# A gated delta rule woven by hand into the projections of one encoder layer

## The chip, the core and the metric

The kernel runs on one core of a Trainium2 chip. The metric is device time of one execution in microseconds (us). The kernel before takes 2366.16 us, the median of three runs (2364.62 to 2370.51).

## The reference, cut to what matters

The program is a two-layer encoder for two groups of rows, 256 and 512, that share all weights; side by side they make T = 768 columns of 1024 features. The first (even) layer normalises, projects, runs three branches (a Hyena long convolution, a gated DeltaNet in both directions with 8 heads of 128, an attention over a memory) and projects back; the second (odd) layer has attention branches and is not touched. What matters here is the DeltaNet and the input projections that feed it and the Hyena branch:

```python
qkv = silu(centred_depthwise_conv(z_qkv, gdn_conv_w))        # 5 taps
q = l2_normalize(q) * d ** -0.5;  k = l2_normalize(k)
# per head and direction, in chunks of 64 rows
a = where(strict, einsum('id,jd->ij', k * beta, k) * decay, 0)
t_inv = triangular_solve(a + eye, eye)                       # unit lower triangle
u, w = t_inv @ (v * beta), t_inv @ (k * beta * exp(g))
# scan over the chunks
v_new = u_i - w_i @ state
o_i = (q_i * exp(g)) @ state + qk_i @ v_new
state = state * exp(g_last) + k_decayed_i.T @ v_new
y_b = rms_norm(o_forward + o_backward, gdn_norm_g) * silu(g_gdn)
# Hyena's share of the projections: 3 taps, then gates
x0, x1, v_hy = split(centred_depthwise_conv(z_hy, hy_conv_w) + hy_conv_b)
y_a = x0 * long_conv(v_hy * x1) * silu(g_hy)
```

## The kernel before, in words

The even layer's middle part holds 64 projections: 32 for the DeltaNet (q, k, v and gate of 8 heads) and 32 for Hyena (x0, x1, v and gate of 8 column blocks). One projection gives 128 features by 768 columns. It runs 8 steps over the 1024 inputs; in each step three products (high x high, low x high, high x low: L256, L258, L260) go over 512 and then 256 columns, so it has 48 products. In this text an eighth is one such step of six products. A projection's output lies in a PSUM tile `pp` of two banks; there are two such tiles. All small products share four more banks, the tiles `pb`.

After its projection q, k and v go through five taps on VectorE (L455: eight instructions, two for each of four taps, after a first one on ScalarE at L448) and a silu; the gate and one Hyena projection of four have a silu alone (L328); the other Hyena projections have four tap instructions. The silu or the last tap frees the `pp` tile.

For each head there are four pieces of small work:

- front: 18 transposes (L332), norms, six products of 256 columns (L554) from which `P` and `A` are scaled (L558), and a gather of `A`'s diagonal blocks over DRAM into `B` and `W` (L572 to L575).
- inverse: 30 steps on VectorE, two instructions each (L589, L591), each dependent on the last; then a copy of `B` (L592) and a scatter over DRAM (`wd`) into `TTN` by 16 transfers (L596, L602).
- levels: the inverse is widened from 32 to 64 to 128 rows on TensorE with evacuations between (L618, L620, L625, L627, L629, L636, L638, L642).
- scan and output: four steps for four chains (two directions, two row groups); in each `v` (L667, L670), `wv` and `w2` (L678, L680, L684), the output and the state (L686 to L693), then six transposes.

The string `ORDER` fixes in which order the pieces are written: F is the projections of a head, its front and its inverse; B is levels and scan; X and U are two Hyena projections each. The order on each engine is not this one: a list scheduler places every instruction by priority and an own estimate of when its inputs are ready, and so mixes small products between the projection's products, at the grain of a single product. At run time every engine takes its instructions strictly in the order so fixed and waits where an input is late.

Of the kernel before, what the change touches and what calls it, by code (L numbers as in the profile page):

```python
# [18 lines left out]
T = 768  # L19
# [204 lines left out]
ORDER = "F0 X0 F1 U0 B0 X1 F2 U1 B1 X2 F3 U2 B2 X3 F4 U3 B3 X4 F5 U4 B4 X5 F6 U5 B5 F7 X6 B6 U6 B7 X7 U7"  # L224


class K:
# [216 lines left out]
    def conv(self, out, ps, taps, tile_ix, width, bias=None):  # L444
# [13 lines left out]

# [25 lines left out]

    def gdn_proj(self, p, h, n0):
        we = self.a["we"]
        kq = p.tile([128, 2, T], F32, tag="kq", name="kq", bufs=2)
        for i, nm in enumerate(("q", "k", "v")):
            w = self.wload(we[n0 + i], self.wp, 128)
            ps = self.proj(w)  # L490
            acc = p.tile([128, T], F32, tag="cv", name="cv", bufs=2)
            self.conv(acc, ps, V_GCW, 8 * i + h, 5)
            if nm == "v":
                vT = p.tile([128, T], F32, tag="vt", name="vT")
                dst = vT
# [4 lines left out]
        ps = self.proj(w)  # L500
        sg = p.tile([128, T], F32, tag="sg", name="sg", bufs=2)
        self.silu2(p, sg, ps)
        return kq, vT, sg

    def gdn_front(self, p, h, E, kq, vT, sg):
# [8 lines left out]
        for which in range(2):  # L514
            sqs = p.tile([128, 128], F32, tag="vs", name="sqs")
            for t0, n in ((0, 4), (4, 2)):
# [6 lines left out]
                if which == 0:  # L523
                    nc.scalar.activation(out=kt[:, t0:t0 + n, :], in_=v3, func=AF.Copy)
        nc.vector.tensor_scalar_add(ss, ss, 4.0 * EPS)
# [14 lines left out]
        for t0, n in ((0, 4), (4, 2)):  # L540
            pt = self.bank()
            for t in range(n):
                self.transpose(pt[:, 128 * t:128 * t + 128], vT[:, 128 * (t0 + t):128 * (t0 + t) + 128])
            nc.vector.tensor_tensor(out=nv[:, t0:t0 + n, :], in0=pt[:, :128 * n].rearrange("p (t d) -> p t d", t=n),
                                    in1=nk[:, t0:t0 + n, None].to_broadcast([128, n, 128]), op=ALU.mult)

        self.mark("g.AP%d" % h)
        Pm = p.tile([128, 2, TT, 128], F32, tag="P", name="P", bufs=2)
        for t0 in range(0, TT, 2):
# [7 lines left out]
            for o, x, e in ((Pm[:, 0, t2], 1, E[0][:, t2]), (Pm[:, 1, t2], 1, E[1][:, t2]), (A[:, t2], 0, A[:, t2])):  # L557
                nc.vector.tensor_tensor(out=o, in0=v[:, :, x], in1=e, op=ALU.mult)  # L558

# [17 lines left out]
        return dict(kq=kq, sg=sg, kt=kt, nv=nv, rs=rs, ed=ed, A=A, Pm=Pm)  # L577

    def gdn_inv(self, p, h):
# [6 lines left out]
        for m in range(1, 31):  # L586
# [4 lines left out]
            nc.vector.tensor_tensor(out=W[:, :m, m + 1:], in0=W[:, :m, m + 1:], in1=tmp, op=ALU.add)  # L591
        nc.scalar.activation(out=B, in_=W.rearrange("p a b -> p b a"), func=AF.Copy)  # L592
# [11 lines left out]
    def gdn_back(self, p, h, kq, sg, kt, nv, rs, ed, A, Pm):  # L604
# [11 lines left out]
        for t in range(TT):  # L616
            for d, e, l in els:
                mm(ps[sl(l), 32 * t:32 * t + 32], A[sl(e), t, sl(l)], tn[d][sl(e), t, sl(e % 2)], tile_position=(32 * e, 32 * l))  # L618
        x = p.tile([128, TT, 64], F32, tag="x64", name="x32", bufs=1)
        nc.vector.tensor_scalar_mul(x[:, :, :32], tv(ps, 32), -1.0)  # L620
        pd = [self.bank() for _ in range(2)]
        for t in range(TT):
# [3 lines left out]
            for d, e, l in (els[0], els[3]):  # L626
                mm(pd[d][sl(l), c], tt[d][sl(l), t, sl(l)], x[sl(l), t, :32], tile_position=(32 * l, 32 * l))  # L627
        for d, e, l in (els[0], els[3]):
            nc.vector.tensor_copy(tn[d][sl(l), :, sl(e % 2)], tv(pd[d], 32)[sl(l)])  # L629
        for d, e, l in els:  # L630
            nc.scalar.activation(out=tt[d][sl(e), :, sl(l)], in_=tv(pd[d], 32)[sl(e)], func=AF.Copy)
        hf = [(0, slice(0, 64), slice(64, 128)), (1, slice(64, 128), slice(0, 64))]
        ps = self.bank()
        for t in range(TT):
            for d, eq, lq in hf:
                mm(ps[lq, 64 * t:64 * t + 64], A[eq, t, lq], tn[d][eq, t, :], tile_position=(eq.start, lq.start))  # L636
        x = p.tile([128, TT, 64], F32, tag="x64", name="x64", bufs=1)
        nc.vector.tensor_scalar_mul(x, tv(ps, 64), -1.0)  # L638
        ps = self.bank()
# [3 lines left out]
        for d, eq, lq in hf:  # L643
            nc.scalar.activation(out=tt[d][eq, :, lq], in_=tv(ps, 64)[eq], func=AF.Copy)
        yield
# [11 lines left out]
        for step in range(4):  # L657
            for si, (d, seq) in enumerate(seqs):
                if step >= len(seq):
                    continue  # L660
                t = seq[step]
                ts = slice(128 * t, 128 * t + 128)
                if step == 0:
                    v1 = nv[:, t, :]
                else:
                    ps = self.bank()
                    mm(ps[:, :128], kq[:, 0, ts], S[si])  # L667
                    mm(ps[:, 128:256], kq[:, 1, ts], S[si])
                    v1 = p.tile([128, 128], F32, tag="v1", name="v1", bufs=3)
                    nc.vector.scalar_tensor_tensor(out=v1, in0=ps[:, :128], scalar=self.gneg[:, d, t, h:h + 1], in1=nv[:, t, :], op0=ALU.mult, op1=ALU.add)  # L670
                    eg = self.gex[:, 3 * d, t, h:h + 1]
                    if t not in seen:
                        nc.scalar.activation(out=o[:, t, :], in_=ps[:, 128:256], func=AF.Copy, scale=eg)
                        seen.add(t)
                    else:
                        nc.vector.scalar_tensor_tensor(out=o[:, t, :], in0=ps[:, 128:256], scalar=eg, in1=o[:, t, :], op0=ALU.mult, op1=ALU.add)
                ps = self.bank()
                mm(ps[:, :128], TTN[:, d, t, 0:128], v1)  # L678
                w = p.tile([128, 128], F32, tag="wv", name="wv", bufs=2)
                nc.vector.tensor_copy(w, ps[:, :128])  # L680
                last = step == len(seq) - 1
                if not last:
                    w2 = p.tile([128, 128], F32, tag="w2", name="w2", bufs=2)
                    nc.scalar.activation(out=w2, in_=ps[:, :128], func=AF.Copy, scale=ed[:, d, t:t + 1])  # L684
                ps = self.bank()
                mm(ps[:, :128], Pm[:, d, t, :], w)  # L686
                if not last:
                    mm(ps[:, 128:256], kt[:, t, :], w2)
# [12 lines left out]
                yield  # L701

# [9 lines left out]
        y = sg  # L712
        for t0, n in ((0, 4), (4, 2)):
# [4 lines left out]
            nc.vector.scalar_tensor_tensor(out=y[:, cs], in0=pt[:, :128 * n], scalar=self.vec(V_GN), in1=sg[:, cs], op0=ALU.mult, op1=ALU.mult)  # L718
        nc.scalar.dma_start(out=self.y[8 + h], in_=y)


    def hy_proj(self, p, c, n0, halves=(0, 1)):
        nc = self.nc

        def part(i):
            w = self.wload(self.a["we"][n0 + i], self.wp, 128)
            ps = self.proj(w)
            t = p.tile([128, T], F32, tag="hy", name="hy", bufs=2)
            if i < 3:
                self.conv(t, ps, V_HCW, 8 * i + c, 3, bias=self.vec(V_HCB + 8 * i + c))  # L730
            else:
                self.silu2(p, t, ps)
            return t
        for i, j, dst in [((1, 2, self.ud[c]), (0, 3, self.xd[c]))[x] for x in halves]:
            t0, t1 = part(i), part(j)
            nc.gpsimd.tensor_tensor(out=t1, in0=t1, in1=t0, op=ALU.mult)
            nc.scalar.dma_start(out=dst, in_=t1)

# [611 lines left out]
def trunk(tc, a, outs, dbg=None):  # L1350
    nc = tc.nc
    dbg = dbg or {}
    with ExitStack() as ctx:
# [24 lines left out]
        with ExitStack() as gd:  # L1378
# [32 lines left out]
            def front(i):  # L1411
                if i > 0:
                    E = k.gdn_decay(p, i)
                k.mark("gproj")
                g = k.gdn_proj(p, i, 4 * i)
                if i == 0:
                    k.mark("gates")
                    k.gdn_gates(p)
                if i == 0:
                    E = k.gdn_decay(p, 0)  # L1420
                st[i] = k.gdn_front(p, i, E, *g)
                k.gdn_inv(p, i)

            def hy(c, halves=(0, 1)):
                k.mark("hproj")
                k.hy_proj(p, c, 32 + 4 * c, halves)
            def back(i):
                st["o", i] = k.gdn_back(p, i, **st.pop(i))
                for _ in range(13):
                    next(st["o", i])  # L1430

            def out(i):
                for _ in st["o", i]:
                    pass
            run = {"F": front, "B": back, "U": lambda c: hy(c, (0,)), "X": lambda c: hy(c, (1,))}
            for ch in ORDER.split():
                i = int(ch[1])
                run[ch[0]](i)
                if ch[0] == "B" and i < 7:
                    out(i)  # L1440
# [4 lines left out]
            def hyconv():  # L1445
# [4 lines left out]
                out(7)  # L1450
# [113 lines left out]
```

## Time and profile before

| what | value |
|---|---|
| median of three runs | 2366.16 us |
| profiled execution | 2362.44 us |
| its span | 2360.7 us (1.7 us lie around it) |
| TensorE busy | 2213.2 us, 94% |
| VectorE busy | 1414.8 us, 60% |
| ScalarE busy | 896.5 us, 38% |
| GpSimd busy | 433.9 us, 18% |

Shares are means over the whole span. The part that the change touches lies between about 273 and 1051 us of the span; the rows further down are from there. A busy TensorE may run at a granted clock of 0.50 instead of 1.00, so its waits and its clock have both to be read.

### The profile page before, as it was taken

The numbers are of one execution on the slowest core, as the hardware profiler recorded it, in microseconds if no ns is written. First come the engines' busy times: TensorE is split into PE (matmuls) and PEld (weight loads), VectorE is DVE, ScalarE is ACT, GpSimd is POOL, SyncE is SP. The second block draws the span as 40 slices with busy tenths as digits, with TensorE's granted clock in tenths as the row PEclk, the third lists the DMA queues.
The fourth block names the chain that finished last, engine by engine and source line by source line (L and its number), as shares of the span: only waits on it lengthen the run. The fifth ranks groups of instructions, "written<-read, shape, count | busy, mean of one in ns | idle before, by whom it ended". The sixth has DMA issues, their size and how long they took to land. (4 is left out here: it accounts for less than half of the span.)

```text
span 2360.7 us, 35185 instructions
## 1 busy us (share of the span) xinstructions
PE 2213.2 (94%) x13648; PEld 1855.1 (79%) x13648; DVE 1414.8 (60%) x3236; ACT 896.5 (38%) x1888; POOL 433.9 (18%) x303
## 2 busy tenths in 40 slices
PE   8999898889999998889999979999999999999897
PEld 6788776777878887777778858988888877778785
DVE  6775387785776867758651264236555577664414
ACT  6333544435345344322142352122222344443423
POOL 2344242223233231223300140000000000000002
PEclk9999999999999998999999989999999999999898
DMA  7442223222223222246362342111111211111613
GB/s 247 138 158 96 73 84 78 82 82 73 78 73 90 78 62 60 67 165 222 113 197 62 102 135 90 54 56 58 52 46 43 77 50 50 40 62 46 203 63 107
DMA packets 122705, 218.98 MB, mean 93 GB/s; under 512 B 49592, under 2 KB 62297, under 8 KB 122282
## 3 DMA queue, kind: packets, MB, share of 16 engines
q1 hardware_dynamic: 102746, 171.86, 23.9%
q10 hardware_dynamic: 19568, 44.04, 5.0%
q8 instruction: 107, 1.75, 0.3%
q0 software_dynamic: 224, 0.83, 0.1%
q14 instruction: 60, 0.49, 0.1%
HBM read 174.43 MB, written 42.25 MB: 92 GB/s over the span
## 5 line engine op out<-in xcount | busy, mean ns | idle before, releaser
L256 PE MATMUL pp<-hhi,w 128*128 128x512 f32 (+1 forms) x2032 | 558.5, 348 | 20.5 <-DVE cv L455 9.6
L258 PE MATMUL pp<-hlo,w 128*128 128x512 f32 (+1 forms) x2032 | 553.6, 347 | 0.0
L260 PE MATMUL pp<-hhi,w 128*128 128x512 f32 (+1 forms) x2032 | 545.9, 344 | 0.0
L256 PEld LDWEIGHTS pp<-hhi,w 128*128 128x128 f32 (+1 forms) x2032 | 321.2, 190 | 68.3 <-issue 17.2
L258 PEld LDWEIGHTS pp<-hlo,w 128*128 128x128 f32 (+1 forms) x2032 | 319.4, 190 | 47.9 <-issue 6.6
L260 PEld LDWEIGHTS pp<-hhi,w 128*128 128x128 f32 (+1 forms) x2032 | 318.0, 189 | 44.8 <-issue 2.7
L1013 PE MATMUL pp<-yh,wo 128*128 128x256 f32 (+1 forms) x1152 | 274.1, 348 | 17.3 <-DVE wo L241 9.0
L240 ACT ACTIVATE w<-wr 128x1024 fp32r<-128x1024 f32 x155 | 163.3, 1053 | 296.6 <-PE pp L260 247.3
L241 POOL TENSOR_TENSOR w<-wr,w 128x1024 fp32r<-128x1024 f32 (+1 forms) x65 | 155.3, 2389 | 462.5 <-ACT w L240 305.4
L1013 PEld LDWEIGHTS pp<-yh,wo 128*128 128x128 f32 x1152 | 191.5, 195 | 48.8 <-ACT yh L240 11.5
L241 DVE TENSOR_TENSOR w<-wr,w 128x1024 fp32r<-128x1024 f32 x90 | 113.6, 1263 | 140.3 <-ACT w L240 140.1
L241 DVE TENSOR_TENSOR wo<-wor,wo 128x640 fp32r<-128x640 f32 (+1 forms) x76 | 62.0, 817 | 191.5 <-ACT wo L240 191.4
L1013 PE MATMUL pp<-yl,wo 128*128 128x512 f32 (+1 forms) x576 | 170.2, 349 | 0.2
L241 POOL TENSOR_TENSOR xk<-raw,xk 128x512 fp32r<-128x512 f32 x8 | 10.8, 1356 | 751.7 <-ACT xk L240 751.7
L455 DVE SCALAR_TENSOR_TENSOR cv<-pp,vecs,cv 128x510 f32<-128x510 f32 (+1 forms) x192 | 107.4, 605 | 24.7 <-ACT cv L448 24.7
L1013 PEld LDWEIGHTS pp<-yl,wo 128*128 128x128 f32 x576 | 100.1, 194 | 17.3 <-DVE yl L241 1.9
L240 ACT ACTIVATE wo<-wor 128x640 fp32r<-128x640 f32 (+1 forms) x76 | 52.0, 686 | 159.1 <-PE pp L1013 146.4
L589 DVE TENSOR_TENSOR Bt<-W,B 48x30 f32<-48x30 f32 (+14 forms) x240 | 98.5, 410 | 4.2 <-DMA B<-bd 2.5
L591 DVE TENSOR_TENSOR W<-W,Bt 48x30 f32<-48x30 f32 (+14 forms) x240 | 97.9, 408 | 1.8
L1022 POOL TENSOR_TENSOR oacc<-oacc,osq 128x768 f32<-128x768 f32 (+2 forms) x15 | 24.0, 1601 | 279.6 <-ACT osq L1018 279.6
L455 DVE SCALAR_TENSOR_TENSOR hy<-pp,vecs,hy 128x511 f32<-128x511 f32 x96 | 55.6, 606 | 30.6 <-ACT hy L448 30.2
L686 PE MATMUL pb<-wv,P 128*128 128x128 f32 x192 | 42.4, 303 | 20.9 <-DVE wv L680 20.9
(322 smaller groups left out, 3736.4 us busy)
## 6 DMA issues: line engine op xcount, KB each, us to landing
wr<-we SPq DMA_DIRECT2D x72, 512.0 KB, 3.5
wr<-wog SPq DMA_DIRECT2D x30, 512.0 KB, 3.6
wor<-weo SPq DMA_DIRECT2D x40, 320.0 KB, 3.2
wr<-wqk SPq DMA_DIRECT2D x24, 512.0 KB, 3.3
wor<-woo SPq DMA_DIRECT2D x36, 256.0 KB, 3.0
yr<-ye SPq DMA_DIRECT2D x20, 384.0 KB, 3.9
dec<-dec ACTq DMA_DIRECT2D x8, 768.0 KB, 4.3
fd<-F ACTq DMA_DIRECT2D x8, 768.0 KB, 3.5
```

Source lines behind the costliest of these rows:

```text
L240: nc.scalar.activation(out=hi, in_=src, func=AF.Copy)
L241: (lo_eng or self.lo_eng or nc.vector).tensor_tensor(out=lo, in0=src, in1=hi.bitcast(F32), op=ALU.subtract)
L256: mm(ps[:, s:e], wh, rhs_hi[:, s:e], start=first, stop=False)
L258: mm(ps[:, s:e], wh, rhs_lo[:, s:e], start=False, stop=False)
L260: mm(ps[:, s:e], wl, rhs_hi[:, s:e], start=False, stop=last)
L455: nc.vector.scalar_tensor_tensor(out=out[:, lo:hi], in0=ps[:, lo + s:hi + s], scalar=self.vec(taps + 24 * j + tile_ix), in1=out[:, lo:hi], ...
L589: nc.vector.tensor_tensor(out=tmp, in0=W[:, :m, m:m + 1].to_broadcast([48, m, n]), in1=B[:, m:m + 1, m + 1:].to_broadcast([48, m, n]), op= ...
L591: nc.vector.tensor_tensor(out=W[:, :m, m + 1:], in0=W[:, :m, m + 1:], in1=tmp, op=ALU.add)
L686: mm(ps[:, :128], Pm[:, d, t, :], w)
L1013: mm(ps[:, s:e], w[:, wi, j, :], y[order[i], g], start=i == 0 and x == 0, stop=i == nk - 1 and x == 2)
L1022: nc.gpsimd.tensor_tensor(out=acc[:, s:e], in0=acc[:, s:e], in1=sq[:, s:e], op=ALU.add)
```

## The change

`ORDER` goes. The projections become a generator (`big`) that stops after each eighth; the taps, the inverse and the small work become generators too. One loop runs `big`; after each eighth it deals out two instructions of taps or silu from a queue (`k.post`), one inverse step of each head whose inverse has begun, and small groups of products at a rate of six per five eighths. TensorE's order is then exactly the order in which the loop writes (`tc.manual_schedule`); the other engines stay with the scheduler. The levels and the scan of head i-1 follow directly on the front of head i. The scan is regrouped: in each step all chains' `v`, then all `wv`, then all outputs and states. Some buffers grow (`kq` 2 to 3, `v1` 3 to 4, `wv` and `w2` 2 to 4); `pp` and `pb` don't. Each engine has the same instructions as before; only their order differs.

```diff
-ORDER = "F0 X0 F1 U0 B0 X1 F2 U1 B1 X2 F3 U2 B2 X3 F4 U3 B3 X4 F5 U4 B4 X5 F6 U5 B5 F7 X6 B6 U6 B7 X7 U7"
+    def proj_g(self, whl):
+        ps = self.pp.tile([128, 1024], F32, tag="pp", name="pp")[:, :T]
+        for k in range(8):
+            self.mm3(ps, whl, 0, self.hhi[k], self.hlo[k], k, k == 0, k == 7, ((0, 512), (512, 768)))
+            yield
+        return ps
...
+        for i, nm in enumerate(("q", "k", "v")):
+            w = self.wload(we[n0 + i], self.wp, 128)
+            ps = yield from self.proj_g(w)
+            self.post.append(post(i, nm, ps))
...
+        for i, j, dst in ((0, 3, self.xd[c]), (1, 2, self.ud[c])):
+            ts = []
+            for x in (i, j):
+                ps = yield from self.proj_g(self.wload(self.a["we"][n0 + x], self.wp, 128))
+                ts.append(p.tile([128, T], F32, tag="hy", name="hy", bufs=2))
+                self.post.append(post(x, ps, ts[-1]))
+            self.post.append(gate(*ts, dst))
...
+            def small():
+                for i in range(8):
+                    while i not in fronts:
+                        yield
+                    E, q = fronts.pop(i)
+                    sg = q.pop("sg")
+                    st[i] = dict((yield from k.gdn_front(p, i, E, **q)), sg=sg)
+                    inv.append(k.gdn_inv(p, i))
+                    if i > 0:
+                        yield from k.gdn_back(p, i - 1, **st.pop(i - 1))
+                for _ in inv[7]:
+                    yield
+                yield from k.gdn_back(p, 7, **st.pop(7))
+
+            def big():
+                hys = chain(*(k.hy_proj(p, c, 32 + 4 * c) for c in range(8)))
+                for i in range(8):
...
+                    q = yield from k.gdn_proj(p, i, 4 * i)
...
+                    while "sg" not in q:
+                        run(k.post)
+                    fronts[i] = E, q
+                    if i > 0:
+                        for _ in range(24):
+                            next(hys)
+                            yield
+                yield from hys
...
+            with tc.manual_schedule(engines={mybir.EngineType.PE}):
+                for n, _ in enumerate(big()):
+                    if n % 8 == 7:
+                        while len(k.post) > 2:
+                            run(k.post)
+                    run(k.post)
+                    run(k.post)
+                    for g in inv:
+                        next(g, None)
+                    while done < n * 6 // 5:
+                        done += 1
+                        next(sm, None)
```

Lines shift with the new code: L455 becomes L462, L589 and L591 become L609 and L611, L618 becomes L639, L625 becomes L648, L636 becomes L662, L678 becomes L710, L686 becomes L726, L256 to L260 become L255 to L259, L328 becomes L335.

Three places show what moves. The first is TensorE where the levels of head 0 begin (L618, later L639). Before, they stand in the ninth projection after the small products of the gates (`pp_3625`):

```order
L258 MATMUL pp_3625<-hlo_364,w_3622 128x512
L258 MATMUL pp_3625<-hlo_364,w_3622 128x256
L618 MATMUL pb_3305<-TTN0_1973,A_2446 32x32
L260 MATMUL pp_3625<-hhi_356,w_3622 128x512
L260 MATMUL pp_3625<-hhi_356,w_3622 128x256
```

After, they stand behind the fifth (`pp_2833`), two eighths after the last product of the front of head 1 (L573):

```order
L573 MATMUL pb_2981<-kq_2398 128x256 x2
L573 MATMUL pb_2987<-kq_2398 128x256 x2
...
L259 MATMUL pp_2833<-hhi_356,w_2830 128x512
L259 MATMUL pp_2833<-hhi_356,w_2830 128x256
L639 MATMUL pb_3037<-TTN0_1973,A_2501 32x32 x24
L255 MATMUL pp_3068<-hhi_349,w_3065 128x512
```

So four projections fewer stand between the gates and the first use of `TTN`. The second place is VectorE around a Hyena gate, which has a silu alone. Before, the silu that frees `pp_4728` stands among the inverse steps, ahead of all taps of the next head:

```order
L591 TENSOR_TENSOR W_4142<-W_4142,Bt_4144 48x20x11
L328 SCALAR_TENSOR_TENSOR hy_4777<-th_4778,pp_4728 128x768
L589 TENSOR_TENSOR Bt_4144<-W_4142,B_1971 48x210
L693 SCALAR_TENSOR_TENSOR S0_4581<-S0_4515,gex_2347,pb_4578 128x128
```

After, the like silu (`pp_4220`, made just ahead of q, k, v and gate of head 3: `pp_4372`, `pp_4496`, `pp_4633`, `pp_4742`) stands behind the taps of all three and behind the gate's silu:

```order
L462 SCALAR_TENSOR_TENSOR cv_4749<-pp_4633,vecs_66,cv_4749 128x254
L335 SCALAR_TENSOR_TENSOR vT_4794<-th_4795,cv_4749 128x768
L761 SCALAR_TENSOR_TENSOR sg_2824<-pb_4769,vecs_66,sg_2824 128x512
...
L335 SCALAR_TENSOR_TENSOR sg_4816<-th_4817,pp_4742 128x768
L335 SCALAR_TENSOR_TENSOR hy_4820<-th_4833,pp_4220 128x768
L543 TENSOR_SCALAR ss_4838<-ss_4838 128x12
```

So one of the two `pp` tiles stays taken through four projections; the same comes once more, with `pp_8144` and head 7. The third place is TensorE in the scan. Before, five or six of a projection's products lie between the product that `wv` is copied from (L678) and the one that reads `wv` (L686):

```order
L678 MATMUL pb_3529<-v1_3526,TTN0_1973 128x128
L258 MATMUL pp_3768<-hlo_362,w_3765 128x512
...
L260 MATMUL pp_3768<-hhi_354,w_3765 128x512
...
L256 MATMUL pp_3768<-hhi_355,w_3765 128x512
L686 MATMUL pb_3535<-wv_3531,P_2458 128x128
L667 MATMUL pb_3542<-S2_3505,kq_1977 128x128
```

After, two whole eighths and the other chain's product lie between them (`pb_3552` gives `wv_3554`):

```order
L710 MATMUL pb_3552<-v1_3505,TTN0_1973 128x128
L255 MATMUL pp_3513<-hhi_352,w_3510 128x512
...
L710 MATMUL pb_3568<-v1_3529,TTN0_1973 128x128
L255 MATMUL pp_3513<-hhi_353,w_3510 128x512
...
L725 MATMUL pb_3585<-w2_3556,kt_2411 128x128
L726 MATMUL pb_3585<-wv_3554,P_2525 128x128
```

What moved here: more projection work now lies between each small product and the next that needs its evacuated result.

## Rows read from the trace of the kernel before

**Rows 1.** View by windows: us, busy time of each engine, granted clock, DMA

```profile
240.00:1040.00 800.00, 728.29 (x5427) 621.07 (x5426) 560.42 (x1580) 354.13 (x897) 220.00 (x103) 0.97 0.27 78
```

**Rows 2.** TensorE's waits from 240 to 1040: total, times, longest

```profile
PE pb L686 <- DVE wv L680: 20.9, 18, 2.5
PE pb L678 <- DVE v L670: 10.0, 12, 1.7
PE pp L256 <- DVE cv L455: 9.6, 3, 5.2
PE pb L636 <- DVE TTN L629: 8.6, 4, 2.3
PE pp L256 <- DVE hy L455: 7.9, 1, 7.9
```

**Rows 3.** One line at a time: duration min/median/max, first and last start

```profile
L618 PE MATMUL pb<-TTN,A x384: 190/191/213, 374.5 to 1007.1; 32*32 32x32 f32 x192
...
L905 PE MATMUL pp<-g,Y x192: 272/378/797, 1051.0 to 1181.3; 128*128 128x257 f32 x128, 128*128 128x129 f32 x64
```

**Rows 4.** Timeline, products of a projection and of the scan: start, duration

```profile
562.20 0.51 PE L256 MATMUL pp<-hhi,w 128*128 128x512 f32 x2
...
563.24 0.51 PE L256 MATMUL pp<-hhi,w 128*128 128x512 f32 x2
...
889.84 0.39 PE L667 MATMUL pb<-S,kq 128*128 128x128 f32 x2
890.07 0.39 PE L688 MATMUL pb<-w,kt 128*128 128x128 f32 x2
```

**Rows 5.** Timeline of the start, from front to scatter of head 0

```profile
273.33 0.88 PE L332 MATMUL pb<-cm,kq 128*128 128x128 f32 x6
...
300.51 1.09 DVE L558 TENSOR_TENSOR A<-pb,A 128x256 f32<-128x256 f32 x3 [3.64 <-POOL A L539]
...
316.62 0.69 DVE L589 TENSOR_TENSOR Bt<-W,B 48x30 f32<-48x30 f32 x1
...
359.46 1.92 ACT L592 ACTIVATE B<-W 48x1024 f32<-48x1024 f32 x1
...
363.52 0.46 SPq L602 DMA_DIRECT2D TTN<-wd  x1
```

**Rows 6.** The page's costliest groups: the two inverse instructions

```profile
L589 DVE TENSOR_TENSOR Bt<-W,B 48x30 f32<-48x30 f32 (+14 forms) x240 | 98.5, 410 | 4.2 <-DMA B<-bd 2.5
...
L591 DVE TENSOR_TENSOR W<-W,Bt 48x30 f32<-48x30 f32 (+14 forms) x240 | 97.9, 408 | 1.8
```

**Rows 7.** Timeline, taps that follow each other, and a wait for taps

```profile
307.71 0.88 ACT L448 ACTIVATE cv<-pp,vecs 128x768 f32<-128x768 f32 x1
...
308.62 4.28 DVE L455 SCALAR_TENSOR_TENSOR cv<-pp,vecs,cv 128x510 f32<-128x510 f32 x8 [3.12 <-ACT cv L448]
...
426.48 0.77 PE L256 MATMUL pp<-hhi,w 128*128 128x512 f32 x1 [5.21 <-DVE cv L455]
```

**Rows 8.** Timeline, front of head 3 and the levels behind it

```profile
541.80 1.47 PE L332 MATMUL pb<-cm,kq 128*128 128x128 f32 x12
...
558.09 1.09 DVE L558 TENSOR_TENSOR A<-pb,A 128x256 f32<-128x256 f32 x3 [1.51 <-POOL A L539]
...
561.69 0.99 DVE L569 TENSOR_TENSOR bt<-bt,nmask 128x384 f32<-128x384 f32 x1
...
571.59 0.33 PE L636 MATMUL pb<-TTN,A 64*64 64x64 f32 x2 [2.27 <-DVE TTN L629]
```

**Rows 9.** View by windows: inverse and scan lie side by side

```profile
578.00:614.00 36.00, 32.74 (x214) 28.77 (x214) 34.54 (x108) 12.11 (x34) 6.84 (x3) 1.00 0.12 41
```

**Rows 10.** View by windows, a stretch behind a wait

```profile
422.00:427.00 5.00, 0.53 (x1) 0.50 (x2) 5.00 (x14) 0.99 (x2) 2.50 (x1) 0.62 0.14 29
```

**Rows 11.** Timeline, an inverse step beside GpSimd

```profile
585.66 2.39 POOL L241 TENSOR_TENSOR w<-wr,w 128x1024 fp32r<-128x1024 f32 x1 [12.57 <-ACT w L240]
...
585.77 2.52 DVE L591 TENSOR_TENSOR W<-W,Bt 48x210 f32<-48x210 f32 x1
```

More of the change, by code (lines that the diff above doesn't have):

```diff
@@ L442, in gdn_gates, with conv_g @@
         self.gc, self.beta, self.gex, self.gneg = gc, beta, ex, neg
-    def conv(self, out, ps, taps, tile_ix, width, bias=None):
+    def conv_g(self, out, ps, taps, tile_ix, width, bias=None):
         nc = self.nc
@@ L657, in gdn_back @@
         for step in range(4):
[L658 to L661, printed above, removed]
+            live = [(si, d, seq[step], step == len(seq) - 1) for si, (d, seq) in enumerate(seqs) if step < len(seq)]
+            v1s, ws = {}, {}
+            for si, d, t, last in live:
                 ts = slice(128 * t, 128 * t + 128)
                 if step == 0:
-                    v1 = nv[:, t, :]
-                else:
[L666 to L676, printed above, removed]
@@ new lines, in gdn_back @@
+                    v1s[si] = nv[:, t, :]
+                    continue
+                ps = self.bank()
+                mm(ps[:, :128], kq[:, 0, ts], S[si])
+                mm(ps[:, 128:256], kq[:, 1, ts], S[si])
+                v1 = v1s[si] = p.tile([128, 128], F32, tag="v1", name="v1", bufs=4)
+                nc.vector.scalar_tensor_tensor(out=v1, in0=ps[:, :128], scalar=self.gneg[:, d, t, h:h + 1], in1=nv[:, t, :], op0=ALU.mult, op1=ALU.add)
+                eg = self.gex[:, 3 * d, t, h:h + 1]
@@ L677, in gdn_back @@
+                if t not in seen:
+                    nc.scalar.activation(out=o[:, t, :], in_=ps[:, 128:256], func=AF.Copy, scale=eg)
+                    seen.add(t)
+                else:
+                    nc.vector.scalar_tensor_tensor(out=o[:, t, :], in0=ps[:, 128:256], scalar=eg, in1=o[:, t, :], op0=ALU.mult, op1=ALU.add)
+                yield
+            if 0 < len(live) < 4 and step:
+                yield
+            for si, d, t, last in live:
                 ps = self.bank()
-                mm(ps[:, :128], TTN[:, d, t, 0:128], v1)
@@ L679, in gdn_back @@
-                w = p.tile([128, 128], F32, tag="wv", name="wv", bufs=2)
+                mm(ps[:, :128], TTN[:, d, t, 0:128], v1s[si])
+                w = p.tile([128, 128], F32, tag="wv", name="wv", bufs=4)
                 nc.vector.tensor_copy(w, ps[:, :128])
-                last = step == len(seq) - 1
+                w2 = None
                 if not last:
-                    w2 = p.tile([128, 128], F32, tag="w2", name="w2", bufs=2)
+                    w2 = p.tile([128, 128], F32, tag="w2", name="w2", bufs=4)
@@ L684, in gdn_back @@
                     nc.scalar.activation(out=w2, in_=ps[:, :128], func=AF.Copy, scale=ed[:, d, t:t + 1])
+                ws[si] = w, w2
+                yield
+            if len(live) < 4:
+                yield
+            for si, d, t, last in live:
+                w, w2 = ws[si]
                 ps = self.bank()
+                if not last:
+                    mm(ps[:, 128:256], kt[:, t, :], w2)
                 mm(ps[:, :128], Pm[:, d, t, :], w)
                 if not last:
-                    mm(ps[:, 128:256], kt[:, t, :], w2)
@@ L701, in gdn_back @@
                 yield
+            if len(live) < 4:
+                yield
         self.mark("g.out%d" % h)
@@ L712, in gdn_back @@
         y = sg
+        for _ in range(4):
+            yield
         for t0, n in ((0, 4), (4, 2)):
@@ L1409, in trunk @@
             st = {}
[L1411 to L1440, printed above, removed]
+            k.post, inv = [], []
@@ new lines, in run @@
+            def run(q):
+                if q and next(q[0], k) is k:
+                    q.pop(0)
+            sm, done = small(), 0
+            with tc.manual_schedule(engines={mybir.EngineType.PE}):
[10 more added lines that the diff above has]
+                        next(sm, None)
+                while k.post:
+                    run(k.post)
+                for _ in sm:
+                    for g in inv:
+                        next(g, None)
@@ L1449, in hyconv @@
                     f = k.hy_fwd(p2, 0)
-                out(7)
                 yield
```

66 lines of the change are left out of this document (44 added, 22 removed).

## The prediction, with its working

> **What bounds the kernel now.** I read, in this order, the granted clock and busy time of the touched part, TensorE's waits in it, the first and last start of one line per head, and then single stretches of the timeline. TensorE is busy for 728.3 of 800 us at a mean granted clock of 0.97 [rows 1]. Its waits make up the other 71.7 us: most come in the scan, where products wait for `wv` (20.9 us) and `v` (10.0 us), the rest from taps that free a projection's tile late (9.6 and 7.9 us) and from the levels (8.6 us) [rows 2]. A clock of 0.97 instead of 1.00 costs 0.03 x 800 = 24 us. So the part is bound by TensorE, with 96 us in 800 that no product fills. The levels begin at 374.5 us for head 0 and 1007.1 us for head 7 [rows 3], a period of 632.6 / 7 = 90.4 us. A like share of this, 90.4 x 96 / 800 = 10.8 us, is wait or low clock, so 79.6 us is packed work.
>
> A projection's products follow each other at three pairs in 1.04 us [rows 4]: an eighth takes 1.04 us, a projection 8.33 us. From order, 394.6 eighths lie between the first levels of head 0 and of head 7, 56.4 for a head: 58.7 us, leaving 20.9 us of small products per head.
>
> **The change, part by part.** Instructions stay the same, so nothing is won but from those 96 us; what is lost comes from where the work now stands. I sum from the beginning of head 0's levels.
>
> Packed time first. After the change 72 eighths stand ahead of head 0's levels instead of 104, then 380 to head 7's, then 60. The levels of head 0 need inverse and scatter of head 0. In the rows of before its transposes stand at 273.3, `A` at 300.5, the inverse runs from 316.6 to 359.3 with taps and head 1's front between its steps, and the scatter's 16 transfers start at 363.5 [rows 5] and the levels at 374.5. After, VectorE has the same k, v taps, silus and front of head 1 to do there, so I take 373; at best the inverse begins at the same time and its 60 instructions at 0.41 us, 24.6 us a head [rows 6], with only v's taps between them end near 343, which gives 358; at worst 380. TensorE has 5 projections and two fronts to do in that time, before it had 9, and no other work may pass the waiting product, as the order is fixed. That is 4 projections of 8.33 us, 33 us, done later instead, less 1.5 us: 32 us (17 to 39). They are not added below, as they are in what is left to do from there.
>
> From there the packed sum is 380 x 1.042 = 396 us of projections and 7 x 20.9 = 146 us of small work, then 60 x 1.042 = 63 us and some 16 us of head 7's small work (its front is done): 621 us, from 373 to 994. Before, this end stands at 1051.0 [rows 3]. With no wait at all and a full clock the change would thus give 57 us. Against that stand five terms.
>
> The held tile. Two times one `pp` tile stays taken through q, k, v and gate of a head, so each of these, and the projection behind, begins only when the tile of the last is free. After q, k or v that is 0.9 us on ScalarE and 4.28 us for eight taps, with the hand-overs 5.4 us [rows 7]; the row of a wait for taps shows 5.21 us of TensorE standing still for just this [rows 7]. Among q's taps stand eight inverse instructions of 0.41 us (some 2 us more of them fall into the wait), so 7.5; behind the gate's silu some 2. Together 7.5 + 5.4 + 5.4 + 2 = 20 us; VectorE uses them for inverse and scan that it would otherwise be late with, so I count 17, twice: **+34 us** (24 to 39). There is work enough in the program to hide it, but it is fixed behind the waiting product.
>
> Front and levels. The levels now follow the front of the next head. Their first part needs two `pb` tiles; three of the four are held by products that wait for `A`, which ends 559.18 - 541.80 = 17.4 us after the first transposes, held up by ScalarE and GpSimd [rows 8]. TensorE reaches that place after 9 eighths, transposes and `P` products, 9.4 + 5.6 = 15 us: it waits 3 to 4 us with the evacuation that follows. Then the copies into `TTN` stand on VectorE behind the gather's transposes (561.69 + 0.99 is their end in the row [rows 8]) and the levels' next part waits 2 us or more; before, 29.8 us after the first transposes, that wait was 2.27 us [rows 8]. 6 us for each of 6 heads: **+36 us** (3 to 8 each).
>
> Scan on VectorE. Before, one stretch has inverse and scan side by side: VectorE is busy for 34.54 of 36 us [rows 9]. After, order counts 103 instructions on VectorE from the inverse's first to its last, before 105, but eight taps more (4.28 / 8 = 0.54 us each [rows 7]) and some ten copies and sums less (at the row's mean, 34.54 / 108 = 0.32 us): 34.5 + 4.3 - 3.2 = 35.6 us. Beside them stand about 21 eighths and 40 scan products on TensorE, 21.9 us and, at 890.07 - 889.84 = 0.23 us each [rows 4], 9.2 us: 31.1 us. The scan's waits of before (31 us in all) go, since two eighths are 2.1 us against the longest wait of 2.5; this one comes in their place: some 4 us for each of the five heads without a held tile, **+20 us** (0 to 6 each).
>
> SP's queue, clock and end. The scatter's 16 issues keep SP for up to 374.5 - 363.5 = 11 us, and a weight load behind them waits; a projection of 8.33 us and the second weight tile cover it, so I count nothing (0 to 3 a head where the cover is gone). Behind a wait the granted clock was 0.62 over 5 us [rows 10], a loss of 1.9 us. Some eight long waits: +10 us (0 to 25). The end, with 7.5 projections beside head 7's inverse and scan where before 1.5 stood, is the packed one with **+5 us** (0 to 10).
>
> The sum: 994 + 34 + 36 + 20 + 10 + 5 = 1099, against 1051: +48 us on the profiled 2362.4 us, which lies 3.7 us under the median; on the median 2414 us.
>
> **The rivals.** First, the weave does what its regularity suggests: in a cycle nearly no wait is left. For it speaks that the scan's 31 us and the taps' 17.5 us [rows 2] have the shape of small products that come too soon after their inputs; against it, that the front's chain of 17.4 us through three engines lies ahead of the levels as before. With half the held tile's price, 17 us, 2 us for each of 7 heads and nothing else the end is 994 + 17 + 14 = 1025: -26, 2340 us. By the Trainium skill's page Perfetto Trace Analysis, section Optimization Strategy, a kernel whose most contended engine changes over time may gain from interleaving those regimes; that speaks for this rival, and the row of VectorE at 34.54 of 36 us beside its mean of 70% shows that there are such regimes.
>
> Second, a balance: half of the front's and of the scan's terms, no clock, 26 us for the held tiles, give 994 + 26 + 28 + 3 = 1051, no change, 2366 us. For it speaks that VectorE is busy for 560.4 of 800 us, 70% [rows 1], so that a wait can be made up later; against it, that TensorE's order can't make up for a wait.
>
> Third, much slower: VectorE falls behind and the waits pile up. It is one mechanism: taps, inverse, `TTN` copies and scan evacuations are one queue on VectorE, and an instruction of it stands still beside GpSimd: an inverse step took 2.52 us beside a weight split of 2.39 us, against a mean of 0.41 us [rows 11, 6]. TensorE waits for it in all places at once and at half clock. With the upper ends of the terms above (start 7 later, held tiles 39, front 48, scan 6 for 7 heads, clock 25, end 10): 994 + 7 + 39 + 48 + 42 + 25 + 10 = 1165, +114, 2480 us. It decides from the point at which VectorE's work for a head passes TensorE's: 77 us packed. By the Trainium skill's page TensorE: Matmul & The Clock Gate, section What's actually happening, the slow state is the default and activity releases it; the stretch at 0.62 behind a wait agrees.
>
> That the change does nothing is out, since order shows other places on every engine.
>
> **How the numbers follow.** The forecast has 0.66 (2380 to 2460 its own range), the first rival 0.13, the balance 0.10, the third 0.11. A measurement tells 0.3%, 7 us, from no change. Faster than 2359 us: 0.13; within: 0.07, most of the balance; slower: 0.80. The range leaves a tenth at each end: below it ends within the balance's lower side, 2355, above near the third rival, 2475.
>
> **What would show it.** In the profile after, the first levels stand at 358 to 380 us with one or two projections' time of waiting ahead of them; then two stretches, at the projections of head 3 and of head 7, where TensorE waits three times some 5 us for taps; and in every head a wait of 3 us or more between the levels' first products. The scan's waits for `wv` should be nearly gone. The last levels should start at about 373 + 542 + 90 = 1005 us, as late as before, but with 60 eighths still to do. The prediction is wrong if the levels' period (first to last start by 7) is under 85 us, if no wait for taps stands at the two held tiles, or if head 0's levels start under 350 us.

## The result and the profile after

The changed kernel takes 2475.01 us (median of four runs, 2468.89 to 2479.07) against 2365.39 us of the kernel before on the same chip: a ratio of 1.046 (95% interval 1.043 to 1.049), 110 us slower. Slower was right; 2414 us was not, and the median lies at the very end of the range, 0.01 us beyond its 2475.

The page's first lines, with the first and last start of the levels (L618 before, L639 now) and of the work behind the touched part:

```profile
PE 2236.9 (91%) x13648; PEld 1884.2 (76%) x13648; DVE 1432.9 (58%) x3236; ACT 893.7 (36%) x1888; POOL 432.6 (18%) x303
...
L639 PE MATMUL pb<-TTN,A x384: 190/191/255, 371.2 to 1067.6; 32*32 32x32 f32 x192
...
L954 PE MATMUL pp<-g,Y x192: 272/378/485, 1161.7 to 1292.0; 128*128 128x257 f32 x128, 128*128 128x129 f32 x64
```

What lies behind the touched part begins at 1161.7 instead of 1051.0 us [rows 3] and lasts as long as before, so the whole 110.7 us lie between. TensorE has the same instructions, yet is busy for 2236.9 us instead of 2213.2: 24 us more are products at the lower clock; the other 87 us of the span's 110.8 are waiting.

TensorE's waits from 240 to 1160 us (total, times, longest), beside [rows 2]:

```profile
PE pp L255 <- DVE cv L462: 36.1, 6, 8.9
PE pp L255 <- DVE Bt L609: 21.9, 2, 11.0
PE pb L639 <- DMA TTN<-wd: 20.0, 2, 19.3
PE pb L648 <- DVE A L577: 15.4, 6, 3.0
...
PE pb L725 <- ACT w L716: 8.6, 8, 1.8
PE pb L710 <- DVE v L698: 7.1, 7, 2.7
...
PE pb L726 <- DVE wv L712: 2.2, 2, 1.1
```

The scan's wait for `wv` fell from 20.9 to 2.2 us, as the regrouping promised. The waits for taps grew from 17.5 to 58 us (the 21.9 under an inverse instruction are taps too: its neighbour in VectorE's queue came last). The levels of the eight heads start at 371.2, 460.9, 585.7, 677.7, 771.5, 866.3, 987.5 and 1067.2 us. So the periods are 89.7, **124.8**, 92.0, 93.7, 94.8, **121.2** and 79.7 us: two long ones, at the projections of heads 3 and 7, where a tile is held. One of them by windows (busy time, granted clock), and its waits for taps on the timeline:

```profile
461.00:586.00 125.00, 91.88 (x677) 80.16 (x676) 71.66 (x197) 43.81 (x113) 26.84 (x13) 0.84 0.20 57
```

```profile
507.23 2.49 POOL L240 TENSOR_TENSOR w<-wr,w 128x1024 fp32r<-128x1024 f32 x1 [10.28 <-ACT w L239]
...
507.55 2.37 DVE L611 TENSOR_TENSOR W<-W,Bt 48x184 f32<-48x184 f32 x1
...
516.08 0.98 PE L255 MATMUL pp<-hhi,w 128*128 128x512 f32 x2 [10.97 <-DVE Bt L609]
...
548.49 2.34 POOL L240 TENSOR_TENSOR w<-wr,w 128x1024 fp32r<-128x1024 f32 x1 [15.68 <-ACT w L239]
...
548.63 2.22 DVE L751 SCALAR_TENSOR_TENSOR so<-so,rs 128x6 f32<-128x6 f32 x1
...
551.75 4.27 DVE L462 SCALAR_TENSOR_TENSOR cv<-pp,vecs,cv 128x510 f32<-128x510 f32 x8
...
556.17 0.98 PE L255 MATMUL pp<-hhi,w 128*128 128x512 f32 x2 [8.91 <-DVE cv L462]
```

To be seen: the projection starts right after the eighth tap of the one before (551.75 + 4.27 = 556.02 us, then 556.17); ahead of the taps an instruction on six columns takes 2.22 us beside GpSimd's split of 2.34 us (a split makes the low half of a weight); and the first two products behind each wait take 0.98 us where 0.51 is usual [rows 4].

### The profile page after: what moved, and what is told of

Read it like the earlier page. It is cut to its first block, busy times and chain, and to the rows that moved or that the text cites. A ratio compares the mean times of both kernels' runs of the same rounds, so it can differ in the third digit from the quotient of the medians.

```text
span 2471.5 us, 35188 instructions
## 1 busy us (share of the span) xinstructions
PE 2236.9 (91%) x13648; PEld 1884.2 (76%) x13648; DVE 1432.9 (58%) x3236; ACT 893.7 (36%) x1888; POOL 432.6 (18%) x303
## 3 DMA queue, kind: packets, MB, share of 16 engines
q8 instruction: 107, 1.75, 0.3%
## 5 line engine op out<-in xcount | busy, mean ns | idle before, releaser
L255 PE MATMUL pp<-hhi,w 128*128 128x512 f32 (+1 forms) x2032 | 583.8, 366 | 69.6 <-DVE cv L462 36.1
L259 PE MATMUL pp<-hhi,w 128*128 128x512 f32 (+1 forms) x2032 | 544.4, 347 | 0.0
L255 PEld LDWEIGHTS pp<-hhi,w 128*128 128x128 f32 (+1 forms) x2032 | 326.3, 196 | 110.4 <-issue 64.9
L259 PEld LDWEIGHTS pp<-hhi,w 128*128 128x128 f32 (+1 forms) x2032 | 322.2, 194 | 49.2 <-issue 2.7
L240 POOL TENSOR_TENSOR xk<-raw,xk 128x512 fp32r<-128x512 f32 x8 | 10.8, 1356 | 752.2 <-ACT xk L239 752.2
L462 DVE SCALAR_TENSOR_TENSOR cv<-pp,vecs,cv 128x510 f32<-128x510 f32 (+1 forms) x192 | 106.8, 606 | 17.6 <-ACT cv L455 17.5
L609 DVE TENSOR_TENSOR Bt<-W,B 48x30 f32<-48x30 f32 (+14 forms) x240 | 100.2, 418 | 3.2 <-DMA W<-bd 0.4
L611 DVE TENSOR_TENSOR W<-W,Bt 48x30 f32<-48x30 f32 (+14 forms) x240 | 99.3, 414 | 3.1
L462 DVE SCALAR_TENSOR_TENSOR hy<-pp,vecs,hy 128x511 f32<-128x511 f32 x96 | 54.9, 607 | 19.4 <-ACT hy L455 19.2
L712 DVE COPY wv<-pb 128x128 f32<-128x128 f32 x96 | 26.3, 282 | 60.5 <-PE pb L710 60.5
```

Source lines behind the costliest of these rows:

```text
L240: (lo_eng or self.lo_eng or nc.vector).tensor_tensor(out=lo, in0=src, in1=hi.bitcast(F32), op=ALU.subtract)
L255: mm(ps[:, s:e], wh, rhs_hi[:, s:e], start=first, stop=False)
L259: mm(ps[:, s:e], wl, rhs_hi[:, s:e], start=False, stop=last)
L462: nc.vector.scalar_tensor_tensor(out=out[:, lo:hi], in0=ps[:, lo + s:hi + s], scalar=self.vec(taps + 24 * j + tile_ix), in1=out[:, lo:hi], ...
L609: nc.vector.tensor_tensor(out=tmp, in0=W[:, :m, m:m + 1].to_broadcast([48, m, n]), in1=B[:, m:m + 1, m + 1:].to_broadcast([48, m, n]), op= ...
```

## The experiments

All times are medians beside runs of the kernel before on the same chip (2356 to 2370 us); ratios to it with 95% intervals.

**The two places that looked certain.** `release` frees the tile in time:

```diff
 for k in range(8):
     self.mm3(ps, whl, 0, ...)
+    if k == 7 and last:
+        last(ps)          # puts the Hyena taps or silu into k.post here
     yield
```

> The changed kernel, with one edit: a Hyena projection's taps or silu are put into the queue with its last eighth, not at the next call of the generator, so the two silus that held a projection tile through a whole head come before that head's taps. Theory A (the held tile costs 28.7 us of waits each time, 10.97 + 5.94 + 8.91 + 2.88, and some 8 us of clock, of which a normal period has 4): the two long periods of 124.8 and 118.7 us fall to the 92 to 95 us of the others, 2475 - 55 = about 2420 us, ratio to the kernel before 1.023. Rival B (VectorE is the bound, the tile is only where its backlog shows): the waits come back elsewhere in the same heads, 2455 us or more, ratio over 1.037.

2425.38 us, ratio 1.0263 (1.0247 to 1.0278): 50 us less. Both long periods are gone (464.2 to 559.6 and 847.0 to 941.7 us; the second had been 121.2 us, not the 118.7 of the expectation). The stretch that answers to the one above:

```profile
464.00:560.00 96.00, 84.79 (x691) 73.87 (x690) 71.09 (x198) 43.35 (x115) 26.47 (x13) 0.96 0.25 74
```

With the tile held, TensorE waited 28.7 us for taps each time. Not all of this is won back: here it stands still for 11.2 us (96.00 - 84.79) instead of 33.1 (125.00 - 91.88), 21.9 us less, as some 7 us of waits for `w`, `o` and others come in their place. On top come 7 us of clock (91.88 - 84.79 us busy for the same work). So the two long periods get shorter by 29.4 and 26.5 us, while four of the other five grow by 1.5 to 3 us; over the whole part the scan's waits for `w`, `v`, `wv` and `o` rise from 21.5 to 44.8 us. Mostly theory A, with a part of rival B.

`start` takes away `if i > 0:` ahead of the 24 Hyena eighths, so 8 projections stand ahead of head 0's levels; `rel_start` has both.

> The changed kernel, with one edit: three Hyena projections stand behind head 0's gates, ahead of head 1's projections, so 8 instead of 5 projections stand ahead of the first levels. Theory A (the start loses what TensorE could have done in its 19.3 us wait for the scatter and the waits ahead of it): the wait shrinks to under 8 us, the end comes 22 to 30 us earlier, about 2449 us, ratio 1.035. Rival B (the start's loss is made up later in any case, the end is set by VectorE's heads): within 8 us of 2475.

2453.95 us, ratio 1.0391 (1.0373 to 1.0408): 21 us less, just under theory A; the 19.3 us wait for the scatter is gone. From the first transposes to the first levels TensorE is busy for 88.4 us instead of 63.7 (windows of the changed kernel and of `start`):

```profile
273.00:371.00 98.00, 63.66 (x312) 53.51 (x310) 62.43 (x164) 53.78 (x154) 26.40 (x13) 0.78 0.25 73
```

```profile
273.00:378.00 105.00, 88.41 (x469) 75.26 (x467) 61.78 (x159) 51.47 (x138) 27.58 (x13) 0.89 0.25 75
```

> Both edits together. If the held tile and the start are separate losses, the gains add: 2475 - 55 - 26 = about 2394 us, ratio 1.012. If both are one backlog on VectorE, it is no better than the better of the two alone.

2408.33 us, ratio 1.0191 (1.0167 to 1.0215): 67 of the 71 us. They are separate losses. 45 us against the kernel before remain.

**The fixed order.** `listpe` replaces the manual schedule by nothing; `list_both` is `rel_start` without it.

```diff
-with tc.manual_schedule(engines={mybir.EngineType.PE}):
+with ExitStack():
```

> The changed kernel, but TensorE's order is left to the list scheduler as on the other engines (no manual schedule); the program is written in the same order. Theory A (the fixed order matters little: the program's order already sets which tile is held and when the levels come, and the scheduler goes by that order's priority): 2450 to 2480 us. Rival B (the fixing of TensorE's order is the loss): under 2410 us.

> Both edits (tile released at once, three Hyena projections ahead of head 1), and TensorE's order left to the list scheduler. Theory A (three separate losses: held tile, start, fixed order): the fixed order costs some 5 us in each normal head and 9 in the last, so 2408 - 7 x 5 - 4 = about 2369 us, ratio 1.002. Rival B (the scheduler only undid the held tile and the start in another way): 2395 us or more.

2413.01 us, 1.0208 (1.0192 to 1.0223), and 2391.23 us, 1.011 (1.0077 to 1.0142). Both lie between the theories, 3 and 4 us from rival B. In the changed kernel the fixed order costs 62 us. In the first long period the scheduler puts scan products between the waiting projections: TensorE's waits for taps fall from 28.8 us to 0.3, 17 us of other waits stand there (7.6 for `w` the longest), and the long periods shrink to 111 and 108 us; the first period falls from 89.7 to 75.7 us. With both edits the fixed order costs 17 us. So it is likely that most of what the scheduler won was the held tile and the start, in another way.

**What bounds a normal head.** `half_inv` (on `rel_start`) and its control `before_half` (on the kernel before) leave out every second inverse step:

```diff
 n = 31 - m
+if m % 2 == 0:
+    yield                 # (woven kernel only)
+    continue
```

> Both edits, with every second step of the inverse left out (its result is not the inverse then), 12 us of VectorE less per head. Theory A (in the stretch with the inverse VectorE's queue is the bound, and the scan's waits for o, v and w stand for it): a period falls from 95 to 99 us to 86 or less, 2408 - 7 x 11 = about 2331 us. Rival B (the waits are latencies of front, levels and scan): within 25 us of 2408.

> The kernel before, with every second step of the inverse left out (its result is not the inverse then): the control for the same cut in the woven kernel, which gained 61 us there. Theory A (in the kernel before VectorE is a bound only now and then, as its scheduler puts projection products into the waits): it gains the scan's waits beside the inverse at most, 10 to 30 us, 2335 to 2355 us. Rival B (VectorE is the bound of a head in both kernels alike): 50 us or more, under 2315 us.

2347.72 us, 0.9929 (0.9911 to 0.9946): 61 us less than `rel_start`; and 2322.96 us, 0.9824 (0.9807 to 0.9842): 41 us less than before. The two gains lie in different places. A middle head of `rel_start`, of `half_inv`, and of `before_half`, by windows:

```profile
566.00:665.00 99.00, 86.51 (x641) 75.89 (x642) 72.23 (x197) 42.44 (x112) 26.22 (x12) 0.91 0.25 72
```

```profile
549.00:638.00 89.00, 82.03 (x631) 71.44 (x617) 62.42 (x167) 41.89 (x111) 26.01 (x12) 0.98 0.27 80
```

```profile
547.70:642.90 95.20, 90.86 (x688) 78.37 (x687) 60.51 (x170) 44.53 (x112) 28.62 (x14) 0.98 0.27 81
```

In the woven kernel each of the first six periods falls from 94 to 99 us to 87 to 91, and VectorE's work is all that was taken out. Where it was in the way is seen in the middle head of `rel_start`, while its inverse runs:

```profile
588.00:628.00 40.00, 32.21 (x187) 28.72 (x186) 36.37 (x106) 9.83 (x26) 6.79 (x3) 0.88 0.14 50
```

VectorE is busy for 36.4 of 40 us, and TensorE's waits there are two, for `o` and `w`, 3.9 us each; in the first of them, from 601 to 606 us, VectorE is busy without a gap. With half the inverse the like waits of the period come to 1.9 us, and the scan's waits of the whole part fall from 45.5 to 12.8. Neither kernel waits for the scatter, so it is not the inverse's earlier end that helps. In all, TensorE's waiting in the period falls by 5.5 us and its busy time, with a clock of 0.98 instead of 0.91, by 4.5. In the kernel before, the middle periods give little, from 94 to 98 us to 93 to 95, with TensorE at 90.86 of 95.2; it gains at the start (359.0 instead of 374.5) and in the last two periods (78.6 and 44.7 us instead of 87.9 and 62.2), and loses 13 us again behind them. Its middle heads hold 64 eighths where the woven ones hold 56, in about the same time. The gain lies between the theories.

`before_scan` has one part alone, the regrouped scan in the kernel before:

> The kernel before, with one part of the change alone: the scan written in three passes over the four chains and with v, wv and w2 in four tiles. The scheduler still orders. Theory A (the scan's 31 us of waits for wv and v come from a chain's products standing too near to each other): some 15 us less, 2350 us. Rival B (they come from VectorE's queue beside the inverse, so the grouping changes nothing): 2358 to 2370 us.

2363.56 us, 1.0005 (0.9993 to 1.0016): no change. The waits from 240 to 1040 us show why:

```profile
PE pp L256 <- DVE hy L455: 29.4, 6, 8.1
PE pp L256 <- DVE cv L455: 17.0, 4, 8.2
...
PE pb L678 <- DVE v L669: 3.8, 5, 0.8
```

The scan's 31 us of waits are nearly gone, and the taps' waits have grown from 17.5 to 46.4 us. Both kinds are waits for VectorE. So the likely reading is that the grouping only says which product meets them; what the scheduler's other choices do in this was not tried apart.

**Pace and distance.** On `rel_start`: `rel_start_gap` leaves six small steps empty ahead of the levels, `slow_inv` deals inverse steps in three of four eighths, `rate11` and `rate10` deal `n * 11 // 10` and `n` small groups instead of `n * 6 // 5`, `half_gap` is the gap with half an inverse.

> Both edits, and six of the loop's small steps (five eighths) left empty between a head's front and the levels of the head before. Theory A (the levels follow too close on the front's chain through ScalarE, GpSimd and VectorE): the 18.4 us of waits for A and the clock behind them go, about 2408 - 25 = 2383 us, ratio 1.008. Rival B (VectorE is so late that the scan then waits as much): 2400 us or more.

2416.91 us, 1.0225 (1.021 to 1.024): 9 us more. The waits for `A` became waits for `x` (11.8 us), the evacuation behind it in the levels, and others in front, scan and output.

> Both edits, every second inverse step left out, and five eighths left empty between a front and the levels behind it. With the whole inverse that gap gave nothing (2417 against 2408 us). Theory A (the levels' waits for A, 19.2 us with half the inverse, are a cost of their own once VectorE has time): 2348 - 15 = 2333 us or less. Rival B (the gap only shifts the waits, whatever VectorE does): 2343 us or more.

2355.29 us, 0.9956 (0.9942 to 0.997), 8 us more than `half_inv`: the gap costs, also where VectorE has time. This distance does not remove the levels' waits.

> The woven kernel with both edits (2408 us), the inverse's steps dealt out in three of four eighths, over 40 eighths instead of 30. Theory A (the scan waits since the inverse stands ahead of its evacuations in VectorE's order; there is time left before the scatter is needed): the scan's 41 us of waits for o, v and w halve, 2408 - 25 = 2383 us. Rival B (VectorE's order doesn't change enough, or the inverse then comes late for the levels): 2400 us or more.

2405.95 us, 1.0185 (1.0169 to 1.0201): no change. The scan's waits for `o`, `v` and `w` fell from 40.9 to 32.6 us, and the wait of the output's transposes for `o` rose from 20.6 to 30.1.

> Both edits, the small groups dealt out at 11 per ten eighths instead of 12, so that the scan is spread over some three eighths more. Theory A (beside inverse and taps VectorE needs 36 us and TensorE's order gives it 31): each of 7 heads gains up to 3 us, 2408 - 15 = 2393 us or less. Rival B (VectorE's order moves with it, as when the inverse was dealt out slower): 2400 to 2415 us.

2394.29 us, 1.0128 (1.0101 to 1.0155): 14 us less, a little short of theory A. Spreading the scan helps.

> Both edits, small groups dealt out at one per eighth. A head has some 60 of them against 56 eighths, so the small work falls behind by some four eighths a head. Theory A (the scan's pace against VectorE is the bound of a normal head): another 5 to 10 us, 2385 to 2390 us. Rival B (what falls behind comes back at the end): 2394 us or more.

2463.67 us, 1.0427 (1.04 to 1.0454). Far beyond rival B. Too slow a pace falls behind: periods grow from 100 to 122 us, and from 801 to 1046 us projections wait 36 us, in seven waits, for Hyena's taps and silus.

> Both edits, 11 groups per ten eighths, and TensorE's order left to the list scheduler: what gained so far, together. If the gains add, 2391 - 14 = 2377 us, ratio 1.006; if the scheduler already spreads the scan, 2388 us or more. The kernel before (2364 us) is beaten by neither.

2379.28 us, 1.0075 (1.0052 to 1.0098): the gains add. It is the best of the woven kernels that do the whole work, and still 17 us slower than the one before. What these 17 us are was not tried.

**GpSimd beside VectorE.** `k.lo_eng = nc.vector` puts the weight splits on VectorE, once with both edits (`split_vec`), once in the changed kernel (`held_vec`).

> Both edits, and the weights' low halves are computed on VectorE instead of GpSimd. Theory A (VectorE stands still beside GpSimd: an inverse step of 2.46 us beside a split of 2.60 us, where 0.38 is usual): without GpSimd's splits up to 2 us for each of 7 weights a head come back and 1.26 us each is added, 2390 to 2405 us. Rival B (VectorE's own length counts): 7 x 7 x 1.26 = 62 us of added work on a full queue, 2440 us or more.

2407.22 us, 1.0188 (1.0168 to 1.0208): no change, near theory A; far from the 62 us of rival B.

> The changed kernel with the held tile left as it is, and the weights' low halves computed on VectorE. In the two long periods the waits for q's and v's taps were 10.97 and 8.91 us, 3.5 us each above the sum of what stands there; an inverse instruction of 2.37 us and a small one of 2.22 us stand beside GpSimd's splits. Theory A (those two freezes are the excess): without GpSimd's splits the two waits fall to about 9 and 6.9 us plus what the splits then take on VectorE, and the periods of heads 3 and 7 by 2 to 4 us each, 2467 us. Rival B (the splits of 1.26 us on VectorE take the place of the freezes): 2472 us or more.

2484.54 us, 1.0503 (1.047 to 1.0535): 10 us more, as rival B has it. In the first long period the waits for q's and v's taps fell to 8.50 and 8.00 us and the long periods to 120.7 and 120.1 us, but the normal ones rose to 97 to 101. So the standstill does make up part of those waits, and the splits take as much elsewhere. The Trainium skill's page Perfetto Trace Analysis, section Optimizing Scalar/DVE Operations, says that GpSimd and VectorE share an SBUF read port, so that moving work between them might not help; both runs agree.

**The clock, not settled.** `warm` puts 24, 12 and 20 idle products ahead of the waiting projections of heads 3 and 7.

> The changed kernel, with idle products of 512 columns into a spare small tile ahead of the three projections of heads 3 and 7 that wait for taps (24, 12 and 20 products, less than each wait of 11, 6 and 9 us takes at full clock). Nothing else is filled. Theory A (a wait costs its length and then the low clock behind it): the waits of TensorE lose what the products fill, the end comes 5 to 14 us earlier, since the eighths behind run at full clock: 2461 to 2470 us. Rival B (the clock costs nothing there, since VectorE sets the next wait's end anyway): 2472 to 2478 us.

2473.49 us, 1.0468 (1.0452 to 1.0484): no change, but not a clean test. The products filled only the first half of each wait for taps, and the first two products behind it still ran at the low level:

```profile
516.41 0.98 PE L255 MATMUL pp<-hhi,w 128*128 128x512 f32 x2 [5.55 <-DVE Bt L617]
```

What a full clock would be worth there stays open.

## Why the prediction was wrong

From the first levels to the work behind the part the forecast had 726 us (373 to 1099): 621 of packed work, 95 of waits, 10 of clock. Measured were 790.5 us (371.2 to 1161.7). In them TensorE waits for 120.9 us and is busy for 669.6, at a mean granted clock of 0.92. So the waits were 26 us too small and the busy time 39. Term by term:

- **The start** (371.2 of 373 us): the levels came behind a 19.3 us wait for the scatter. What it costs was put at 32 us, so three of the four lost projections are 24; undoing these three gave 21 and 17.
- **The held tile** (+34 forecast): the largest step that failed among the waits. Place, order and number of waits were right (10.97, 5.94, 8.91 and 2.88 us, twice); the size was not. The raw waits are 28.7 us, not 20, in part since an instruction stands still beside GpSimd ahead of q's and of v's taps (without GpSimd's splits 8.50 and 8.00 us remain of 10.97 and 8.91). I subtracted 3 us for work that VectorE makes up meanwhile; by the windows of `release` it was 7. And 7 us of clock come on top. The two periods fell by 56 us when the tile was freed, and the kernel by 50. The Trainium skill's page Perfetto Trace Analysis, section Matmuls, asks that independent groups rotate through different PSUM banks so that the evacuation of one overlaps the products of the next; with one tile held there is nothing to rotate to, and the trace agrees.
- **Clock** (+10, range to 25): this failed too. The row at 0.62 [rows 10] is nearly all the wait itself, with TensorE busy for 0.53 of 5 us, and not what follows it. Behind that wait the clock was 0.65 from 426.5 to 431.5 us, a loss of 1.75 us: that the 1.9 taken is near is luck. Behind the first wait of 11 us in the changed kernel it was 0.50 for all of 516.1 to 521.1. With the packed sum as corrected in the next point, some 37 us of busy time remain above it, most of them clock (an estimate).
- **Packed work** (621): too small. The share of waits and low clock was taken from 240 to 1040 us, which holds the start. From 374.5 to 1007.1 alone TensorE is busy for 581.8 of 632.6 us at 0.98: 50.8 + 12.7 us, 9.1 per head and not 10.8. That leaves 22.6 us of small products per head instead of 20.9, 12 us in seven heads.
- **Front and levels** (+36): too large. The waits for `A` are 15.4 us and those for `TTN` 3.1. Their mechanism was right, the front's chain, and not VectorE's queue: VectorE itself stands still for GpSimd's product there:

```profile
466.48 1.09 DVE L577 TENSOR_TENSOR A<-pb,A 128x256 f32<-128x256 f32 x3 [2.91 <-POOL A L557]
```

- **Scan** (+20): 21.5 us of waits for `w`, `v`, `wv` and `o`, as forecast, but by luck: with the tile freed they are 44.8 us. What had no term are the output's transposes, which wait 9.7 us for `o`, and 5.0 us for Hyena's taps.
- **The end** (+5): from the last levels to the work behind it passed 94.5 us, some 10 more than forecast. 8.8 us of it are waits, 7.8 of them for inputs of the long convolution that follows (`eu`, `Y`, `R`).

Had only the held tile and the start been wrong, the prediction's own terms without them would give 2414 - 34 - 24 = 2356 us for `rel_start`. It took 2408, so the larger part of the miss stays when both are undone. Part of it is the packed work and the clock above; the rest is the mechanism: the scan's waits there are 45.5 us, and half an inverse takes 61 us off the kernel. Each wait had been priced by itself, as if VectorE had time beside it.

**The third rival** named this mechanism, one queue on VectorE that TensorE meets in several places, and its 2480 us was nearest. The sum is near by luck in part: its front of 48 us and scan of 42 stand against 18.5 and 21.5 of waits, its held tiles of 39 against 57. Its condition was wrong: that VectorE's work for a head must pass TensorE's 77 us. VectorE was busy for 70 to 72 us in each full period but the first (66), and the time came all the same. A mean over a head says too little: in the stretch that has inverse and scan it was at 34.54 of 36 us already [rows 9], and with the order fixed no other product can pass the one that waits.

## What to carry to other kernels

When an order is fixed by hand, sum for each stretch what every engine must do between two points at which the fixed engine waits for it; the longest of these sums is the least that the stretch takes, and chains through several engines, as the front's here, come on top. Idle time elsewhere pays little back: 7 of 28.7 us here. Look where a queue of deferred work is fed across the border of two loops: one late entry held a buffer for a whole head, twice, for 50 us. A regrouping that removes a wait need not remove time: in `before_scan` waits for the same engine came back at other products.

## What the runs showed of the hardware that was not expected

A VectorE instruction on 128 x 6 elements took 2.22 us beside a GpSimd split of 2.34 us, where its neighbours take 0.17; with the splits on VectorE (`held_vec`) all eight instructions of its line took 0.15 to 0.17. Idle products that filled the first half of an 11 us wait, with 5.55 us of wait left behind them, did not bring back the clock of the first two products behind it (0.98 us against 0.51).
